# A pooling-mixer layer on one core: the output weights of three of seven Strassen products stored as float32r pairs when they are folded

## The chip, the cores and the metric

The kernel runs on one core of a Trainium2 chip. Its metric is the device time of one execution in microseconds. TensorE (PE) multiplies matrices, VectorE (DVE), ScalarE (ACT) and GpSimd (POOL) do the element-wise work, and SyncE (SP), like the others, issues transfers between the memory and the on-chip buffers.

## The reference

One layer is computed, of the pooling kind, on x of 4096 frames by 1024 channels, in float32; the final RMSNorm follows.

```python
def trailing_mean(u, window):
    cs = jnp.cumsum(u.astype(jnp.float32), axis=1)
    lagged = jnp.pad(cs, ((0, 0), (window, 0), (0, 0)))[:, :seq]
    ...
    return ((cs - lagged) / count[None, :, None]).astype(u.dtype)

def pool_mixer(h, in_w, group_w, group_b, scale, out_w):
    u, gate = jnp.split(h @ in_w, 2, axis=-1)
    ug = u.reshape(b, s, POOL_GROUPS, POOL_GROUP_DIM)
    pooled = jnp.stack([trailing_mean(ug[:, :, g], w) for g, w in enumerate(POOL_WINDOWS)],
                       axis=2) - ug
    mixed = jnp.einsum('bsgc,gcd->bsgd', pooled, group_w) + group_b
    y = mixed.reshape(b, s, POOL_WIDTH) * scale * jax.nn.silu(gate)
    return y @ out_w

# one layer: h = x + pool_mixer(rms_norm(x)); the result is rms_norm(h)
```

The windows are 2, 4, 8 and 16 frames, one for each group of 256 channels. `in_w` is 1024 x 2048, `out_w` 1024 x 1024.

## The kernel before, in words

**Pairs.** Every float32 operand of a matmul is held as a pair of float32r tiles, a high part (a rounded copy, made on ScalarE) and a low part (the operand less its high part, made on VectorE). A product is the sum of three passes, high by high, high by low and low by high. Making such a pair is called a split; the tiles with the results are called `w` (weights) and `op` (the operand that changes with the block).

**Seven products.** The three big products (values, gate, output) are cut into 2 x 2 quarters and done with seven products instead of eight, P1 to P7 (the scheme of Strassen and Winograd). Each needs a sum or difference of quarters of the weights and of the operand; P1 and P2 take quarters as they are. The weights' sums are made once by `combine` (P5, P4 and P3 among them), stored in memory and loaded where they are used.

**Blocks.** The group maps are multiplied into the value weights at the start, so that what is left of the mixing is the trailing mean. Then come four input blocks of 1024 frames for the first half of the channels ("a", a0 to a3), four for the second half ("b", b0 to b3), each with the values and gates of its channels and with seven products in the order P1, P2, P7, P6, P5, P4, P3; and eight output blocks ("o") of 512 frames, in the order P1, P7, P6, P2, P5, P4, P3. One product of an input block is 48 matmuls of 512 columns and takes 10.4 us; a few products are cut once more into seven smaller ones. The operand sums of later blocks are formed ahead, kept in memory as `sd` (`sd2_1_0` is block 2, P1, first half), loaded into a slot and split into an `op` tile. Beside the products of a block VectorE also adds the banks' results into the quarters, makes the trailing means (a prefix scan, a difference and a scaled subtraction, on `vt` slots with a `window` tile) and gates.

**The output weights.** `load_wo` (L376) loads four raw quarters of one half of `out_w` in b1 and b2. `make_wo` (L381) scales their rows, in step P6 of the same block, and `store_weights` (L303) stores P1 and P2, forms the other five by `combine` and stores those in `wod`, one 512 KB tile for each product and half. This is a fold: the first (half 0) falls into b1, the second (half 1) into b2. In the last input block b3, `load_w` (L387) loads a product's two halves into slots, splits them into its `w` tiles (by then free of the gate's weights) and gives the slots back.

```python
                for p in {P1: (), P2: (), P7: (P1,), P6: (P2, P7), P5: (P6, P5)}.get(i, (i,)):
                    load_w(wod, p)
```

**What sets the order.** There is one instruction queue for each engine, and it runs in order. Which order the instructions stand in is set when the program is built: a scheduler interleaves them by their dependences, `issue_after` ties one behind another, and `InOrder` (L64) keeps the output blocks in the order of the text. Most element-wise work and all DMA issues go through `InOrder.call` and so carry its line, L79, in the profile; the main matmuls carry L799, those of `product_seven` L745, the small leaf products of the mixing L941. Slots are shared: eleven `st`, eight `vt`, four `op`. `take` hands out the one that has been free the longest, and `give` returns it; a tile that is taken again waits for the last reader of the one before.

Of the kernel before, what the change touches and what calls it, by code (L numbers as in the profile page):

```python
# [10 lines left out]
F32 = mybir.dt.float32  # L11
F32R = mybir.dt.float32r
# [3 lines left out]
P = 128  # L16
D = 1024
S = 4096
H = 512
# [12 lines left out]
P1, P2, P3, P4, P5, P6, P7 = range(1, 8)  # L32
# [54 lines left out]
def kernel(  # L87
# [37 lines left out]
    vector, scalar, gpsimd, sync = (  # L125
        InOrder(tc, e) for e in (nc.vector, nc.scalar, nc.gpsimd, nc.sync)
    )
# [5 lines left out]
    dram = ctx.enter_context(tc.tile_pool(name="dram", bufs=1, space=bass.MemoryType.DRAM))  # L133
# [3 lines left out]
    def new_w(i):  # L137
        return [
            mem.tile([P, 2, 2, H], F32R, tag=f"w{i}_{h}", name=f"w{i}_{h}") for h in range(2)
        ]  # L140

    w = {i: new_w(i) for i in (P1, P2, P6, P7)}
# [35 lines left out]
    def take(pattern="p (a b) -> p a b", pool=None, **sizes):  # L178
        sizes = sizes or {"a": 2}
        if pool is None:  # L180
            spare = len(vt.free) > keep[0] or not st.free
            pool = vt if spare and vt.age() < st.age() else st
        return pool.take(lambda t: t[:, 0:D].rearrange(pattern, **sizes))
# [4 lines left out]
    def give(ap):  # L188
        next(p for p in (st, vt, early, early5) if id(ap) in p.used).give(ap)
# [4 lines left out]
    def sub(dst, a, b):  # L194
        return vector.tensor_tensor(out=dst, in0=a, in1=b, op=ALU.subtract)
# [4 lines left out]
    def copy(dst, src, func=AF.Copy):  # L200
        return scalar.activation(dst, src, func)

    def split(dst, src):

        latest_copy[0] = copy(dst[:, 0], src).ins
        latest_split[0] = sub(dst[:, 1], src, dst[:, 0].bitcast(F32)).ins

    latest_split, latest_copy = [None], [None]
# [9 lines left out]
    t3d = [dram.tile([P, 2, H], F32, name=f"t3d{h}") for h in range(2)]  # L218
    wod = {
        i: [dram.tile([P, 2, H], F32, name=f"wod{i}_{h}") for h in range(2)]  # L220
        for i in range(P1, P7 + 1)
    }
    sd = [
        {
# [65 lines left out]
    def combine(b11, b21, b12, b22):  # L290

        sub(b12, b22, b12)
        add(b11, b12, b11)
        sub(b21, b21, b11)
        t1 = take()
        sub(t1, b22, b11)
        return {P6: b11, P7: b12, P5: t1, P4: b21, P3: b22}
# [5 lines left out]
    def store_weights(dst, h, b11, b21, b12, b22):  # L303
        sync.dma_start(out=dst[P1][h], in_=b11)
        sync.dma_start(out=dst[P2][h], in_=b21)
        for i, u in combine(b11, b21, b12, b22).items():
            sync.dma_start(out=dst[i][h], in_=u)
            give(u)


# [65 lines left out]
    def load_wo(h):  # L376
        for n in range(2):
            for kh in range(2):
                raw_wo[kh, n] = load_rows(out_w, 4 * kh + 2 * h, n * H)

    def make_wo(h):  # L381
        us = dict(raw_wo)
        for (kh, n), u in us.items():
            scale_rows(u, pair(scale_c, h, kh))
        store_weights(wod, h, us[0, 0], us[1, 0], us[0, 1], us[1, 1])

    def load_w(src, i):  # L387
        for h in range(2):
            u = take()
            sync.dma_start(out=u, in_=src[i][h])  # L390
            with tc.issue_after(evicted[0]):
                split(w[i][h], u)
            give(u)
# [1274 lines left out]
    def pool_later(n):  # L1668
        kind, b, i = steps[n]
        if i == P4:  # L1670
            args = (b, 0 if kind == "a" else 1, 1, ev.pop("22"), ev.pop("21"))
            wait = int(b == 0) if kind == "a" else 1 if b < NB - 1 else 2
        elif i == P3:
            args = (b, 0 if kind == "a" else 1, 0, ev.pop("12"), ev.pop("11"))
            wait = 1 + int(b == 0) if kind == "a" else 2 if b < NB - 1 else 5
        else:
            return
        pending.append((n + wait, args))

    def pool_due(n):  # L1680
        while pending and pending[0][0] <= n:
            pool(*pending.pop(0)[1])
# [204 lines left out]
    for n in range(2, len(steps)):  # L1887
        kind, b, i = steps[n]
# [78 lines left out]
        if kind in ("a", "b"):  # L1967
            pool_later(n)
            if kind == "a":
                pool_due(n)  # L1970
            if kind == "b" and b == NB - 1:
                for p in {P1: (), P2: (), P7: (P1,), P6: (P2, P7), P5: (P6, P5)}.get(i, (i,)):
                    load_w(wod, p)
            if kind == "b" and b in (1, 2) and i == P7:
                load_wo(b - 1)
            if kind == "b" and b in (1, 2) and i == P6:
                with tc.issue_after(evicted[0]):
                    make_wo(b - 1)
            if kind == "b" and b == NB - 1 and i == P3:
                f = take("p (a b) -> p a b", a=2)  # L1980
                sync.dma_start(
                    out=f.rearrange("p a b -> p (a b)"), in_=final_w.partition_broadcast(P)
                )
                fw.append(f)
# [52 lines left out]
```

## Time and profile before

| what | value |
|---|---|
| median of three runs | 907.41 us (906.5 to 909.38) |
| the profiled execution | 907.14 us |
| its span, first to last instruction | 905.3 us |
| busy TensorE / VectorE / ScalarE / GpSimd | 894.6 / 736.8 / 518.6 / 147.3 us |
| mean granted TensorE clock | 0.998 |
| moved by DMA | 203.30 MB, 225 GB/s on average |

All rows of the profile are from one execution. A row of the table by stretches gives the busy time of each engine in that stretch. A row of the groups gives line, engine, operation, tiles, shape and count, then the sum of busy time and the mean of one, then the idle time of the engine just before them and what ended it. In the rows of a timeline the first number is the start in us from the span's start and the second the time to the end of the row's last instruction; "x3" joins three neighbours. In the rows of DMA issues the last number is the median time from issue to landing.

### The profile page before, as it was taken

What the parts mean: (1) busy time and instruction counts of PE and PEld (TensorE: products, weight loads), DVE (VectorE), ACT (ScalarE), POOL (GpSimd) and SP (SyncE); (2) the same over time, 40 slices, a digit from 0 to 9 for tenths busy, and PEclk for the clock granted to TensorE, in tenths of its full rate; (3) what the DMA queues carried; (4) which work ended last, traced back from release to release, by engine and by line L of the source; (5) the groups of instructions that cost most, each with busy time, mean ns of one, the idle gap of its engine ahead of it and who ended that gap; (6) DMA issues with size and microseconds to landing.
All of it is one profiled execution on the core that took longest, in us unless ns stands there. A gap on an engine that the chain in (4) does not pass through costs nothing.

```text
span 905.3 us, 12421 instructions
## 1 busy us (share of the span) xinstructions
PE 894.6 (99%) x4554; PEld 791.7 (87%) x4554; DVE 736.8 (81%) x910; ACT 518.6 (57%) x848; POOL 147.3 (16%) x244
## 2 busy tenths in 40 slices
PE   9999999999999999999999999999999999999996
PEld 7888888888888888889889889888889898998996
DVE  3899896984996997694596497699898878888798
ACT  7869547446445465346545644855557466565464
POOL 0031110110111000100010011011132343342430
PEclk9999999999999999999999999999999999999999
DMA  9989779677769565245574574756673855945953
GB/s 339 402 313 320 263 279 314 219 299 286 270 248 363 180 236 183 94 163 190 212 244 175 202 262 142 269 188 204 206 220 81 221 176 142 240 143 138 264 179 116
DMA packets 77756, 203.30 MB, mean 225 GB/s; under 512 B 7296, under 2 KB 25088, under 8 KB 77696
## 3 DMA queue, kind: packets, MB, share of 16 engines
q1 hardware_dynamic: 57872, 143.77, 46.0%
q0 software_dynamic: 19104, 57.69, 20.7%
q10 hardware_dynamic: 720, 1.06, 0.3%
q8 instruction: 35, 0.57, 0.3%
q14 instruction: 25, 0.20, 0.1%
HBM read 130.13 MB, written 72.36 MB: 224 GB/s over the span
## 4 chain that ended last, share of the span: by engine, by line
PE 50%; DVE 21%; DMA 10%; issue 6%; ACT 3%; POOL 1%; SPq 0%; DVEq 0%; POOLq 0%; ACTq 0%
PE bank L799 44%; DVE vt L79 8%; DVE st L79 6%; DVE op L79 5%; PE bank L745 3%; DMA vt<-yd 3%; PE bank L941 3%; DMA st<-wvd 2%; ACT op L79 1%; DMA st<-yd 1%; DVE w L79 1%; DMA out<-vt 1%; ACT vt L79 1%; DMA st<-wod 1%; DMA vt<-rd 1%
## 5 line engine op out<-in xcount | busy, mean ns | idle before, releaser
L799 PE MATMUL bank<-op,w 128*128 128x512 f32 x2544 | 550.6, 379 | 0.2 <-ACT st L79 0.2
L799 PEld LDWEIGHTS bank<-op,w 128*128 128x128 f32 x2544 | 480.4, 189 | 68.9 <-ACT st L79 0.6
L799 PE MATMUL bank<-w,op 128*128 128x512 f32 (+1 forms) x1044 | 230.5, 377 | 0.0
L799 PEld LDWEIGHTS bank<-w,op 128*128 128x128 f32 x1044 | 192.3, 189 | 25.0
L79 DVE TENSOR_TENSOR op<-st,op 128x1024 fp32r<-128x1024 f32 x120 | 145.9, 1220 | 60.1 <-ACT op L79 59.7
L79 ACT ACTIVATE op<-st 128x1024 fp32r<-128x1024 f32 x120 | 125.8, 1052 | 86.4 <-PE bank L799 31.2
L79 ACT ACTIVATE op<-vt 128x1024 fp32r<-128x1024 f32 x65 | 68.3, 1053 | 63.0 <-DVE vt L79 40.6
L79 ACT ACTIVATE vt<-bank 128x512 f32<-128x512 f32 (+1 forms) x122 | 67.4, 577 | 43.9 <-PE bank L799 37.8
L79 DVE TENSOR_TENSOR op<-vt,op 128x1024 fp32r<-128x1024 f32 x65 | 78.4, 1218 | 14.2 <-ACT op L79 14.1
L79 DVE TENSOR_TENSOR st<-st,st 128x1024 f32<-128x1024 f32 (+1 forms) x47 | 51.3, 1104 | 31.6 <-ACT st L79 16.8
L79 ACT ACTIVATE bank<-bank 128x512 f32<-128x512 f32 (+1 forms) x84 | 41.1, 490 | 53.1 <-PE bank L799 39.5
L79 POOL COPY vt<-tails 128x32 f32<-128x32 f32 x14 | 17.0, 1219 | 301.4 <-ACT tails L79 130.3
L79 ACT ACTIVATE st<-bank 128x512 f32<-128x512 f32 (+1 forms) x62 | 35.6, 588 | 37.5 <-PE bank L799 22.7
L79 DVE TENSOR_TENSOR vt<-bank,vt 128x512 f32<-128x512 f32 (+1 forms) x90 | 51.3, 596 | 6.0 <-PE bank L941 4.6
L79 ACT ACTIVATE st<-st 128x1024 f32<-128x1024 f32 x34 | 35.8, 1055 | 28.6 <-DVE st L79 27.1
L79 DVE TENSOR_TENSOR st<-bank,st 128x512 f32<-128x512 f32 (+1 forms) x72 | 43.7, 622 | 6.0 <-PE bank L941 3.1
L79 POOL DMA_DIRECT2D sd<-st x45 | 24.0, 535 | 125.1 <-DVE st L79 77.9
L941 PEld LDWEIGHTS bank<-w,op 128*128 128x128 f32 x312 | 40.4, 191 | 1.7
L79 DVE TENSOR_TENSOR st<-st,vt 128x1024 f32<-128x1024 f32 (+1 forms) x34 | 39.1, 1168 | 2.7 <-DMA vt<-rd 2.4
L941 PE MATMUL bank<-w,op 128*128 128x256 f32 x312 | 41.1, 275 | 0.0
L79 DVE TENSOR_TENSOR vt<-vt 128x1024 f32<-128x1024 f32 (+3 forms) x43 | 38.2, 890 | 0.2
L79 DVE TENSOR_TENSOR_SCAN vt<-vt,window 128x1040 f32<-128x1040 f32 x16 | 37.7, 2374 | 0.6 <-DMA wod<-vt 0.5
(118 smaller groups left out, 768.5 us busy)
## 6 DMA issues: line engine op xcount, KB each, us to landing
sd<-st POOLq DMA_DIRECT2D x45, 512.0 KB, 4.2
st<-sd SPq DMA_DIRECT2D x42, 512.0 KB, 4.0
st<-in_xt SPq DMA_DIRECT2D x28, 512.0 KB, 7.4
st<-in_x SPq DMA_DIRECT2D x21, 512.0 KB, 7.9
yd<-st SPq DMA_DIRECT2D x20, 512.0 KB, 3.3
vt<-yd SPq DMA_DIRECT2D x17, 512.0 KB, 10.5
st<-wod SPq DMA_DIRECT2D x16, 512.0 KB, 5.1
out<-vt POOLq DMA_DIRECT2D x16, 512.0 KB, 3.5
```

Of the source, the lines that this page charges most:

```text
L79: r = f(*args, **kwargs)
L745: latest[0] = nc.tensor.matmul(cell(n, c).rearrange("p (a s) -> p a s", s=2), x1, x2, start=i == P1 and k + m == 0, stop=k == 1 and m == 2 ...
L799: latest[0] = nc.tensor.matmul(ps, a, b, start=start and n == 0, stop=stop and n == 2, skip_group_check=True).ins
L941: latest[0] = nc.tensor.matmul(ps, x1, x2, start=start and k + n == 0, stop=k == 1 and n == 2, skip_group_check=True,).ins
```

## The change

In a fold, P5, P4 and P3 no longer go to `wod`. Each sum u is split at once: a slot `high` is taken, ScalarE copies u into it as float32r, VectorE subtracts it from u in place, and both are stored in a new array `pairs_d` (two stores of 512 KB instead of one). In b3, `load_w` for these three is one transfer of 1 MB a half, issued by GpSimd straight into the `w` tile, with no slot, no copy and no subtraction. The table of steps changes too: P5's load goes from step P5 to step P4, P4's from P4 to P3; P3's stays. The matmuls are the same in number and kind; the instructions that make TensorE's program are L814 instead of L799 in the new text.

```diff
@@ -218,7 +218,11 @@
     t3d = [dram.tile([P, 2, H], F32, name=f"t3d{h}") for h in range(2)]
     wod = {
         i: [dram.tile([P, 2, H], F32, name=f"wod{i}_{h}") for h in range(2)]
-        for i in range(P1, P7 + 1)
+        for i in (P1, P2, P6, P7)
+    }
+    pairs_d = {
+        i: [dram.tile([P, 2, 2, H], F32, name=f"pair{i}_{h}") for h in range(2)]
+        for i in (P5, P4, P3)
     }
     sd = [
         {
@@ -304,7 +308,15 @@
         sync.dma_start(out=dst[P1][h], in_=b11)
         sync.dma_start(out=dst[P2][h], in_=b21)
         for i, u in combine(b11, b21, b12, b22).items():
-            sync.dma_start(out=dst[i][h], in_=u)
+            if i in dst:
+                sync.dma_start(out=dst[i][h], in_=u)
+            else:
+                high = take()
+                latest_copy[0] = copy(high.bitcast(F32R), u).ins
+                latest_split[0] = sub(u.bitcast(F32R), u, high).ins
+                for v, t in enumerate((high, u)):
+                    sync.dma_start(out=pairs_d[i][h][:, v], in_=t)
+                give(high)
             give(u)
 
 
@@ -386,6 +398,9 @@
 
     def load_w(src, i):
         for h in range(2):
+            if i not in src:
+                gpsimd.dma_start(out=w[i][h], in_=pairs_d[i][h].bitcast(F32R))
+                continue
             u = take()
             sync.dma_start(out=u, in_=src[i][h])
             with tc.issue_after(evicted[0]):
@@ -1969,7 +1984,7 @@
             if kind == "a":
                 pool_due(n)
             if kind == "b" and b == NB - 1:
-                for p in {P1: (), P2: (), P7: (P1,), P6: (P2, P7), P5: (P6, P5)}.get(i, (i,)):
+                for p in {P1: (), P2: (), P7: (P1,), P6: (P2, P7), P5: (P6,), P4: (P5,), P3: (P4, P3)}[i]:
                     load_w(wod, p)
             if kind == "b" and b in (1, 2) and i == P7:
                 load_wo(b - 1)
```

The order of instructions moves at three places. The first is VectorE behind the first fold, where the end of b1 runs into P1 of b2. In these rows `op3` and `op0` are the two halves of that P1's operand; `st9` and `st1`, `vt3` hold the folded sums. Before:

```order
L79 TENSOR_TENSOR vt6_106<-bank7_76,vt6_106 128x512
L79 TENSOR_TENSOR op2_87<-st5_94,op2_87 128x1024
L79 TENSOR_TENSOR op1_86<-vt4_104,op1_86 128x1024
L79 SCALAR_TENSOR_TENSOR vt3_103<-vt0_100,window_3423 128x1040
L79 SCALAR_TENSOR_TENSOR vt7_107<-vt6_106,window_3432 128x1040
L79 TENSOR_TENSOR st6_95<-bank0_69,st6_95 128x512
L79 TENSOR_TENSOR st6_95<-bank1_70,st6_95 128x512
L79 TENSOR_TENSOR op3_88<-st8_97,op3_88 128x1024
L79 TENSOR_TENSOR st2_91<-bank2_71,st2_91 128x512
L79 SCALAR_TENSOR_TENSOR vt3_103<-vt3_103,vt0_100 128x2x512
L79 TENSOR_TENSOR st2_91<-bank3_72,st2_91 128x512
L79 TENSOR_TENSOR op0_85<-st1_90,op0_85 128x1024
```

After, VectorE in the same stretch:

```order
L79 TENSOR_TENSOR vt3_103<-vt3_103,st8_97 128x1024
L79 TENSOR_TENSOR vt6_106<-bank7_76,vt6_106 128x512
L79 TENSOR_TENSOR op2_87<-st5_94,op2_87 128x1024
L79 TENSOR_TENSOR op1_86<-vt4_104,op1_86 128x1024
L79 SCALAR_TENSOR_TENSOR vt7_107<-vt6_106,window_3441 128x1040
L79 TENSOR_TENSOR st1_90<-st1_90,st8_97 128x1024
L79 TENSOR_TENSOR st6_95<-bank0_69,st6_95 128x512
L79 TENSOR_TENSOR st6_95<-bank1_70,st6_95 128x512
L79 TENSOR_TENSOR st2_91<-bank2_71,st2_91 128x512
L79 SCALAR_TENSOR_TENSOR vt3_103<-vt0_100,window_3432 128x1040
L79 TENSOR_TENSOR st2_91<-bank3_72,st2_91 128x512
L79 TENSOR_TENSOR st9_98<-st9_98,st8_97 128x1024
```

and the ten rows of VectorE that follow these after the change:

```order
L79 SCALAR_TENSOR_TENSOR vt3_103<-vt3_103,vt0_100 128x2x512
L79 SCALAR_TENSOR_TENSOR vt7_107<-vt7_107,vt6_106 128x2x512
L79 SCALAR_TENSOR_TENSOR st6_95<-vt3_103,colt_114,st6_95 128x512 x2
L79 SCALAR_TENSOR_TENSOR st2_91<-vt7_107,colt_114,st2_91 128x512 x2
L79 TENSOR_TENSOR op3_88<-st1_90,op3_88 128x1024
L79 TENSOR_TENSOR op2_87<-vt2_102,op2_87 128x1024
L79 TENSOR_REDUCE window_3570<-vt4_104 128x1
L79 TENSOR_REDUCE window_3579<-vt0_100 128x1
L79 SCALAR_TENSOR_TENSOR vt6_106<-vt4_104,window_3570 128x1040
L79 TENSOR_TENSOR op0_85<-st8_97,op0_85 128x1024
```

The three subtractions with `st8` are new. The halves `op3` and `op0` stood among the evictions of `bank0` to `bank3`, `op0` at the end of the first list. Now both stand in the last list, behind the scaled subtractions of the means (into `st6` and `st2`), and between them are the split of another product's half (`op2`), two reductions and a scan.

The second place is SP's queue in the same stretch, where `sd2_1_0` and `sd2_1_1` are the loads of those two halves and `wod` and `pair` the folded weights. Before:

```order
L79 DMA wod3_0_127<-st9_98 128x1024
L79 DMA wod7_0_135<-st8_97 128x1024
L79 DMA wod6_0_133<-vt1_101 128x1024
L79 DMA st8_97<-sd2_1_0_163 128x1024
L79 DMA wod5_0_131<-vt3_103 128x1024
L79 DMA wod4_0_129<-st1_90 128x1024
L79 DMA st9_98<-sd2_2_1_166 128x1024
L79 DMA vt1_101<-sd2_7_0_175 128x1024
L79 DMA st1_90<-sd2_1_1_164 128x1024
```

After, SP's queue there:

```order
L79 DMA wod7_0_129<-st8_97 128x1024
L79 DMA wod6_0_127<-vt1_101 128x1024
L79 DMA vt1_101<-sd2_7_0_175 128x1024
L79 DMA pair5_0_131<-st8_97 128x1024
L79 DMA pair5_0_131<-vt3_103 128x1024
L79 DMA st5_94<-sd2_6_0_173 128x1024
L79 DMA pair4_0_133<-st8_97 128x1024
L79 DMA pair4_0_133<-st1_90 128x1024
L79 DMA pair3_0_135<-st8_97 128x1024
L79 DMA st1_90<-sd2_1_0_163 128x1024
L79 DMA pair3_0_135<-st9_98 128x1024
L79 DMA st8_97<-sd2_1_1_164 128x1024
```

Both loads now stand behind stores of the pairs. `st8` holds the high parts of all three products in turn, so each copy into it comes after the store before it; it then takes the load of the second half.

The third place is GpSimd's queue at the end of the input blocks, with the six new loads among copies of window tails and ahead of the first additions of x (`in_x`) for the output blocks. After:

```order
L79 COPY vt2_102<-tails_116 128x2x16
L79 DMA w5_0_609<-pair5_0_131 128x2048
L79 COPY vt5_105<-tails_116 128x2x16
L79 DMA w5_1_610<-pair5_1_132 128x2048
L79 COPY vt0_100<-tails_116 128x2x16
L79 DMA w4_0_698<-pair4_0_133 128x2048
L79 DMA w4_1_699<-pair4_1_134 128x2048
L79 DMA w3_0_771<-pair3_0_135 128x2048
L79 DMA w3_1_772<-pair3_1_136 128x2048
L79 DMA st5_94<-in_x 128x512
L79 DMA st9_98<-in_x 128x512
L79 DMA st5_94<-in_x 128x512
```

Before, the copies and additions stood there without the loads between them.

## The prediction

> **What bounds the kernel now.** I read the page's busy times first, then the table by stretches of 25 us, then the list of waits of TensorE.
>
> ```profile
> span 905.3 us, 12421 instructions
> PE 894.6 (99%) x4554; PEld 791.7 (87%) x4554; DVE 736.8 (81%) x910; ACT 518.6 (57%) x848; POOL 147.3 (16%) x244
> ```
>
> TensorE is busy for 894.6 of 905.3 us, and the change touches no matmul. So the time after is 894.6 us plus whatever TensorE then idles, plus 1.8 us outside the span (the profiled execution took 907.14 us, 0.27 below the median 907.41). In the next rows the columns are the length of the stretch, then busy PE, PEld, DVE, ACT, POOL, clock, DMA share and GB/s.
>
> ```profile
> 0.00:25.00 25.00, 23.59 (x126) 18.79 (x127) 10.92 (x18) 17.36 (x30) 0.94 (x5) 1.00 0.94 344
> 450.00:475.00 25.00, 25.00 (x118) 21.89 (x117) 24.86 (x27) 10.27 (x16) 2.33 (x2) 1.00 0.76 257
> 600.00:625.00 25.00, 25.00 (x118) 21.89 (x117) 25.00 (x26) 14.04 (x18) 1.84 (x2) 1.00 0.36 122
> 650.00:675.00 25.00, 23.23 (x125) 20.55 (x124) 23.65 (x34) 16.00 (x29) 8.24 (x18) 1.00 0.67 192
> 875.00:900.00 25.00, 23.01 (x139) 20.89 (x138) 24.26 (x56) 11.91 (x27) 2.87 (x6) 1.00 0.39 140
> ```
>
> ```profile
> PE bank L941 <- DVE vt L79: 1.8, 1, 1.8
> ```
>
> TensorE idles 1.4 us at the start, 1.8 us in 650 to 675 (one wait for VectorE) and 2.0 us in 875 to 900; all after 900 (5.3 us) is the tail. Only the 1.8 us can be won. On the other side VectorE is full in 450 to 475 (24.86 of 25): that is the stretch behind the first fold, into which work is moved. A late VectorE there costs TensorE one for one.
>
> **What is removed.** Six high parts on ScalarE and six low parts on VectorE go from the last input block.
>
> ```profile
> L79 DVE TENSOR_TENSOR w<-st,w 128x1024 fp32r<-128x1024 f32 x25 | 29.6, 1218 | 5.5 <-ACT w L79 5.5
> L79 ACT ACTIVATE w<-st 128x1024 fp32r<-128x1024 f32 x25 | 25.5, 1054 | 6.0 <-DVE st L79 2.4 <-DMA st<-wod 2.1 <-PE bank L799 1.4
> L79 DVE TENSOR_TENSOR st<-st,st 128x1024 f32<-128x1024 f32 x37 | 44.5, 1217 | 30.0 <-ACT st L79 16.8 <-DMA st<-wvd 13.1
> L79 ACT ACTIVATE st<-st 128x1024 f32<-128x1024 f32 x34 | 35.8, 1055 | 28.6 <-DVE st L79 27.1 <-DMA st<-in_x 1.4
> ```
>
> That is 6 x 1.218 = 7.3 us of VectorE and 6 x 1.054 = 6.3 us of ScalarE. Both lie beside matmuls, so they are worth nothing by themselves; they count only as far as they pull the 1.8 us wait at 670 forward. The rows before it:
>
> ```profile
> 612.01 51.96 PE L799 MATMUL bank<-w,op 128*128 128x512 f32 x240
> 644.62 0.69 DVE L79 TENSOR_TENSOR st<-st,st 128x512 f32<-128x512 f32 x1 [1.49 <-DMA st<-wod]
> 645.23 0.68 DVE L79 TENSOR_TENSOR st<-bank,st 128x512 f32<-128x512 f32 x1
> 651.27 2.48 DVE L79 SCALAR_TENSOR_TENSOR st<-st,ors,st 128x1024 f32<-128x1024 f32 x2 [0.63 <-POOL ors L79]
> ```
>
> VectorE waits 1.49 us at 644.62 for an inner weight, and that load's tile came free only after a late split. With VectorE some 7 us ahead this wait goes. But the eviction at 645.23 reads the sixth output product (24 matmuls each), which ends at 612.01 + 144 x 51.96/240 = 643.2, and the row scaling at 651.27 hangs on its sums through GpSimd. So what follows moves forward by at most 1.5 us, not 7: the gain is between 0 and 1.5 us, and I take 1.2.
>
> **What is added at the folds.** Each of the two folds gets three copies (3 x 1.055 = 3.2 us of ScalarE), three subtractions (3 x 1.217 = 3.7 us of VectorE) and three more 512 KB stores. Behind each fold comes P1 of the next input block, whose operand halves are split on VectorE out of slots that the fold held. The trace before, first fold:
>
> ```profile
> 427.04 62.33 PE L799 MATMUL bank<-op,w 128*128 128x512 f32 x288
> ```
>
> ```profile
> 448.27 1.22 DVE L79 TENSOR_TENSOR vt<-st,vt 128x1024 f32<-128x1024 f32 x1
> 449.41 1.88 DVE L79 TENSOR_TENSOR vt<-bank,vt 128x512 f32<-128x512 f32 x3
> 451.21 1.21 DVE L79 TENSOR_TENSOR op<-st,op 128x1024 fp32r<-128x1024 f32 x1
> 453.66 4.68 DVE L79 TENSOR_TENSOR_SCAN vt<-vt,window 128x1040 f32<-128x1040 f32 x2
> 458.26 1.26 DVE L79 TENSOR_TENSOR st<-bank,st 128x512 f32<-128x512 f32 x2
> 459.44 1.21 DVE L79 TENSOR_TENSOR op<-st,op 128x1024 fp32r<-128x1024 f32 x1
> 462.90 1.21 DVE L79 TENSOR_TENSOR op<-st,op 128x1024 fp32r<-128x1024 f32 x1
> 464.04 1.40 DVE L79 SCALAR_TENSOR_TENSOR st<-vt,colt,st 128x512 f32<-128x512 f32 x2
> 465.36 1.22 DVE L79 SCALAR_TENSOR_TENSOR vt<-vt,vt 128x1024 f32<-128x1024 f32 x1
> ```
>
> P6, P5, P4 and P3 are 192 matmuls from 427.04 at 62.33/288 = 0.216 us: P1 starts at 468.5. The rows at 459.44 and 462.90 are its two halves; the second is done at 464.1, 4.4 us ahead. These rows also give VectorE's pace from start to start: 1.14 us for a 1024 operation (448.27 to 449.41), 0.60 for an eviction (three from 449.41 to 451.21), 2.30 for a scan (two from 453.66 to 458.26), 0.66 for a 512 one (two from 464.04 to 465.36).
>
> Now the changed order. From the last sum of the fold (vt3, at 448.27 as before, since nothing ahead of it moves) to the second half of P1's operand, VectorE's queue holds ten 1024 operations (the sum, three new subtractions, the two splits for P3, two subtractions of the window means, the first half of P1, the first half of P2), seven evictions, three scans, four 512 operations and two tiny reductions (0.2 us). That is 11.4 + 4.2 + 6.9 + 2.6 + 0.2 = 25.3 us: the second half starts at 473.5 and is done at 474.8. The first half stands 4.7 us ahead of it (itself, P2's half, the reductions, a scan) and is done at 470.0.
>
> TensorE then goes so. At 468.5 it can do one matmul, on the high part; the next reads the low part of half one, at 470.0: **1.4 us** idle. Eight more matmuls (1.7 us) stand before the first that reads the low part of half two, so it is there at 471.8 and waits until 474.8: **3.0 us** idle. The sum is **4.4 us**, in a queue that cannot be reordered when it runs. So the 4.4 us of slack are used up and as much again is lost, from 3.4 us of subtractions and from a pooling scan and mean that the new order puts ahead of P1's halves.
>
> The loads could add to it. One slot takes the high part of all three products, so each copy waits until the store before it has landed, and the loads of P1's halves stand behind these stores in SP's queue.
>
> ```profile
> 447.53 0.90 SPq L79 DMA_DIRECT2D st<-sd  x1
> 455.61 8.85 SPq L79 DMA_DIRECT2D st<-sd  x4
> ```
>
> ```profile
> wod<-st SPq DMA_DIRECT2D x10, 512.0 KB, 2.8
> st<-sd SPq DMA_DIRECT2D x42, 512.0 KB, 4.0
> sd<-st POOLq DMA_DIRECT2D x45, 512.0 KB, 4.2
> st<-in_x POOLq DMA_DIRECT2D x18, 256.0 KB, 7.5
> ```
>
> Before, the halves were issued at 447.5 and 455.6. Now the first needs the store of P4's low part, issued at 458.2 when the second subtraction ends, and so goes out near 462 and lands near 466; the second needs P3's high part stored, and goes out near 465 and lands near 469. Their copies take 1.05 us each and VectorE reaches the halves at 468.8 and 473.5, so both are just in time. A landing 2 us later than the median would lose up to 1 us at the first half; none can come earlier than VectorE does. I put 4.4 to 6.5 us, and take 4.5.
>
> The second fold has another order: no scan stands between P1's halves there.
>
> ```profile
> 520.03 1.22 DVE L79 TENSOR_TENSOR vt<-st,st 128x1024 f32<-128x1024 f32 x1
> 498.80 62.33 PE L799 MATMUL bank<-op,w 128*128 128x512 f32 x288
> ```
>
> From 520.03 there are six 1024 operations, seven evictions and one scan (6.8 + 4.2 + 2.3 = 13.3 us) to the first half, done at 534.5, and 4.6 us more to the second, done at 539.1. P1 starts at 498.80 + 192 x 0.216 = 540.3 and reads the second half 1.3 us later: 2.5 us to spare, cost 0, or up to 2 us if a store there is slow.
>
> **What is moved to GpSimd's queue.** The six loads are now 1 MB each and wait for TensorE to leave the weight tile. Queued behind them are two copies of window tails and then the residual additions.
>
> ```profile
> 595.07 3.81 POOL L79 COPY vt<-tails 128x32 f32<-128x32 f32 x1 [2.10 <-ACT tails L79]
> 621.02 0.94 POOL L79 DMA_DIRECT2D st<-in_x  x1 [22.13 <-DVE st L79]
> ```
>
> P5's tile is free at 591.3 (612.0 less two products of 10.4), before the copy at 595.07 is due; the last, P3's, is free at 612.0, 9 us ahead of the addition at 621.02. No such transfer of 1 MB is in the trace: twice the 512 KB row of this queue is 8.4 us, and four times the accumulating 256 KB row is 30 us. So P3's lands between 621 and 642 and is read at 643.2; I take the first, since it is a plain copy too. Cost 0. The doubled bytes (3.1 MB more) fall where the DMA share is 0.36.
>
> **The sum**: 907.14 + 4.5 - 1.2 = 910.4, 3.3 us above the profiled execution and 3.0 above the median.
>
> **The rivals.**
> (a) Not slower: P1's halves come in time and the wait at 670 goes. The point is the second half's end: by 469.8 TensorE never waits. For it: before, the same place had 4.4 us to spare, against 3.4 us of added subtractions. Against it: the printed order puts a scan and two means ahead, and VectorE was full there already. Time 907.1 - 1.2 = 905.9.
> (b) Slower by more: the 3.0 us gap grows to over 3.4 us by a late load, or the second fold stalls too, and TensorE's clock drops. The trace shows a slow clock at the very start:
>
> ```profile
> L1687 PE MATMUL bank<-const-bfloat16-1.0 128*128 128x512 bf16 x8 | 3.5, 623 | 0.8 <-PEq L2022 0.8
> ```
>
> Eight matmuls in 3.5 us are 0.44 us each against 0.216: a stretch as long costs 1.8 us. The granted clock was 1.00 in 650 to 675 in spite of the 1.8 us wait. With 2 us of late loads and such a stretch, 910.4 + 2 + 1.8 = 914.2. The Trainium skill, "TensorE: Matmul & The Clock Gate", section "HAM oscillation — how this bites in real kernels", says that idle gaps over about 3.4 us throttle the array again; by that rule the gap forecast here stays just under it, and no run here shows one so long.
> (c) The change doesn't hide its loads: P5's or P3's pair comes late in output block 0. It decides only if a landing takes over 30 us; each us beyond is lost, so 911 to 916.
>
> **How the numbers follow.** The forecast (stall of 4.4 to 6.5 us, gain 0 to 1.5) has 0.63, and its own range is 910 to 913.5. Rival (a) has 0.21, (b) 0.12, (c) 0.04. About 0.3% (2.7 us, so 904.7 to 910.1) is what a measurement can tell from no change. The forecast lies just above its edge: a seventh of it (0.09) falls inside, which with 0.17 of (a) makes 0.26 within, and 0.04 of (a) is left for faster. Slower is 0.54 + 0.12 + 0.04 = 0.70. The range 906 to 914 takes in (a) near its middle and most of (b).
>
> **What would show it.** Right: TensorE waits of about 1.4 and 3.0 us for VectorE's op near 469 and 472, none near 540, and the wait at 670 shorter by 1 us or so; VectorE full from 448 to 477; the loads of the pairs landed before 630. Wrong: no wait of TensorE near 470, or one that a DMA ends; the wait at 670 unchanged; a granted clock below 1.00 behind the gap; TensorE waiting for w in output block 0.

## The result, and the profile after

| | median | range | executions |
|---|---|---|---|
| before | 907.79 us | 906.09 to 910.33 | 10 |
| after | 912.11 us | 910.04 to 912.97 | 10 |

The ratio is 1.0043, 95% interval 1.0029 to 1.0056: 3.9 us slower (2.6 to 5.1); the two medians are 4.3 apart. The profiled execution took 911.34 us, 4.2 more than that of before. Its page begins so:

```profile
span 909.3 us, 12433 instructions
PE 895.9 (99%) x4554; PEld 791.8 (87%) x4554; DVE 736.6 (81%) x910; ACT 519.0 (57%) x848; POOL 150.7 (17%) x250
```

VectorE and ScalarE did as much as before (736.6 us for 736.8, 519.0 for 518.6): the six splits were moved, not saved. The list of TensorE's waits after gives whom it waited for, the us in total, how often, and the longest:

```profile
PE bank L814 <- DVE op L79: 4.0, 2, 2.8
...
PE bank L956 <- DVE vt L79: 0.3, 1, 0.3
```

The wait of 1.8 us at 670 is down to 0.3 (now on L956, the same instruction in the longer text), and two waits for `op` are new. The timeline of TensorE after shows where (in square brackets the idle time ahead of the row and what ended it):

```profile
463.83 4.48 PE L814 MATMUL bank<-op,w 128*128 128x512 f32 x20
469.53 1.99 PE L814 MATMUL bank<-op,w 128*128 128x512 f32 x8 [1.22 <-DVE op L79]
474.35 7.82 PE L814 MATMUL bank<-op,w 128*128 128x512 f32 x35 [2.82 <-DVE op L79]
```

Beside the waits the stall costs a little more: the eight matmuls at 469.53 take 1.99 us where eight at 0.216 take 1.73, and the row at 474.35 begins with such a longer matmul too. Set against the trace of before matmul by matmul, TensorE loses 4.6 us at this place: 4.04 of idle time and 0.27 in the first matmul behind each wait.

The timeline of VectorE after gives the two releasers, the first and the last of these rows, and what stood between the halves:

```profile
468.26 1.22 DVE L79 TENSOR_TENSOR op<-st,op 128x1024 fp32r<-128x1024 f32 x1
469.40 1.22 DVE L79 TENSOR_TENSOR op<-vt,op 128x1024 fp32r<-128x1024 f32 x1
470.53 0.23 DVE L79 TENSOR_REDUCE window<-vt 128x1 f32<-128x8 f32 x2
470.79 2.38 DVE L79 TENSOR_TENSOR_SCAN vt<-vt,window 128x1040 f32<-128x1040 f32 x1
473.09 1.20 DVE L79 TENSOR_TENSOR op<-st,op 128x1024 fp32r<-128x1024 f32 x1
```

The halves that ended at 460.7 and 464.1 before end at 469.5 and 474.3, and none of these rows has idle time ahead of it: VectorE was at work all the while, as the table by stretches has it too.

```profile
448.00:477.00 29.00, 24.96 (x115) 21.23 (x114) 28.97 (x30) 13.11 (x19) 2.39 (x2) 1.00 0.78 271
```

The loads of the pairs, on GpSimd's timeline and among the DMA issues (1 MB, median 7.2 us to landing):

```profile
617.08 0.54 POOL L79 DMA_DIRECT2D w<-pair  x1 [4.64 <-PE bank L814]
625.51 0.91 POOL L79 DMA_DIRECT2D st<-in_x  x1 [7.89 <-DMA st<-yd]
```

```profile
w<-pair POOLq DMA_DIRECT2D x6, 1024.0 KB, 7.2
```

The last one starts when TensorE leaves the tile and delays nothing: the addition behind it waits for another transfer.

### The profile page after: what moved, and what is told of

Read it like the earlier page. It is cut to its first block, busy times and chain, and to the rows that moved or that the text cites. A ratio compares the mean times of both kernels' runs of the same rounds, so it can differ in the third digit from the quotient of the medians.

```text
span 909.3 us, 12433 instructions
## 1 busy us (share of the span) xinstructions
PE 895.9 (99%) x4554; PEld 791.8 (87%) x4554; DVE 736.6 (81%) x910; ACT 519.0 (57%) x848; POOL 150.7 (17%) x250
## 4 chain that ended last, share of the span: by engine, by line
PE 75%; DVE 10%; DMA 7%; issue 4%; ACT 3%; POOL 1%; DVEq 0%; POOLq 0%; ACTq 0%; SPq 0%
PE bank L814 68%; DVE vt L79 4%; PE bank L760 3%; DVE op L79 3%; PE bank L956 3%; DMA vt<-yd 3%; DVE st L79 2%; ACT st L79 1%; DMA st<-yd 1%; PE bank L466 1%; DMA st<-in_x 1%; DMA out<-vt 1%; ACT op L79 1%; ACT vt L79 1%; POOL otmp L79 1%
## 5 line engine op out<-in xcount | busy, mean ns | idle before, releaser
L814 PE MATMUL bank<-op,w 128*128 128x512 f32 x2544 | 550.9, 379 | 4.0 <-DVE op L79 4.0
L814 PEld LDWEIGHTS bank<-op,w 128*128 128x128 f32 x2544 | 480.2, 189 | 73.1 <-DVE op L79 4.8
L814 PE MATMUL bank<-w,op 128*128 128x512 f32 (+1 forms) x1044 | 230.5, 377 | 0.0
L814 PEld LDWEIGHTS bank<-w,op 128*128 128x128 f32 x1044 | 192.3, 189 | 25.0
L79 DVE TENSOR_TENSOR st<-st,st 128x1024 f32<-128x1024 f32 (+2 forms) x51 | 56.1, 1113 | 29.2 <-ACT st L79 16.8
L79 ACT ACTIVATE st<-st 128x1024 f32<-128x1024 f32 (+1 forms) x38 | 40.0, 1057 | 34.3 <-DVE st L79 29.5
L956 PEld LDWEIGHTS bank<-w,op 128*128 128x128 f32 x312 | 40.2, 191 | 2.4 <-ACT bank L79 0.8
L956 PE MATMUL bank<-w,op 128*128 128x256 f32 x312 | 41.3, 275 | 0.1
```

Source lines behind the costliest of these rows:

```text
L79: r = f(*args, **kwargs)
L814: latest[0] = nc.tensor.matmul(ps, a, b, start=start and n == 0, stop=stop and n == 2, skip_group_check=True).ins
L956: latest[0] = nc.tensor.matmul(ps, x1, x2, start=start and k + n == 0, stop=k == 1 and n == 2, skip_group_check=True,).ins
```

## The experiments

The theory, Q: the time is lost in VectorE's queue behind the first fold, because three subtractions come into a stretch that is full, and the new order puts the halves of P1 behind a scan and the means. The rivals: S, the second fold or the loads on GpSimd's queue; L, the loads of the halves behind the stores, in one slot; W, what is added costs TensorE wherever it stands. Each ratio is to the kernel before, run beside it; it is close to that of the medians, not the same.

**e1, pairs in the first fold only.**

```diff
-            if i in dst:
+            if i not in pairs_d or h != 0:
                 sync.dma_start(out=dst[i][h], in_=u)
...
-            if i not in src:
+            if i in pairs_d and h == 0:
                 gpsimd.dma_start(out=w[i][h], ...)
```

> Pairs are made only in the first fold (half 0); half 1 goes through wod and is split in the last input block as before. Theory Q (VectorE's queue behind the first fold is the loss): the order behind the first fold is that of the changed kernel, so TensorE waits 1.2 and 2.8 us for VectorE's op near 469 and 472, as there; half of the relief in the last block is left, so the wait at 670 is 0.3 to 1.8 us. Time 3 to 4.4 us above the kernel before, ratio 1.0033 to 1.0048. Rival S (the second fold, or the loads of pairs on GpSimd's queue with twice the bytes, carry the loss): about half of the loss or less is left, ratio 1.001 to 1.002.

915.62 us, 1.0097 (1.0082 to 1.0111): 8.8 us, twice the expected loss. TensorE's waits:

```profile
PE bank L814 <- DVE op L79: 4.0, 2, 2.8
PE bank L956 <- DVE vt L79: 2.8, 1, 2.8
```

The two waits for `op` are there as expected, so the first fold alone makes them. Two things were not: the wait at 670 grew to 2.8 us, and the clock fell after both waits of 2.8 us. In the table by stretches, cut at the borders of the clock's record, the columns are length, busy PE, PEld, DVE, ACT, POOL, clock, DMA share and GB/s:

```profile
471.94:475.35 3.41, 0.59 (x4) 0.52 (x4) 3.41 (x3) 1.28 (x2) 0.00 (x0) 1.00 0.89 362
475.35:478.77 3.42, 3.42 (x10) 2.70 (x9) 3.42 (x5) 0.58 (x1) 0.00 (x0) 0.50 0.86 303
478.77:482.18 3.41, 3.41 (x18) 2.98 (x17) 3.41 (x5) 0.58 (x1) 0.00 (x0) 1.00 0.81 302
```

A stretch of 3.41 us with 2.82 idle is followed by one at half clock, ten matmuls in place of some sixteen, which costs 1.7 us; then the clock is back. The longer wait at 670 comes from VectorE's wait for an inner weight, 1.49 us before:

```profile
652.85 0.69 DVE L79 TENSOR_TENSOR st<-st,st 128x512 f32<-128x512 f32 x1 [3.59 <-DMA st<-wod]
```

In this trace 4.6 us are lost at the stall, 2.3 more than before around 670, and 3.1 in two stretches at half clock. The profiled execution, at 917.35 us, is the slowest of four: the other three lie at 915.5 to 915.6 with mean clocks of 0.996 and 0.997 in place of 0.994. One halved stretch fewer in these would fit; none of them was traced.

**e2, pairs in the second fold only** (the same edit with `h != 1` and `h == 1`).

> Pairs are made only in the second fold (half 1); half 0 goes through wod as before. Theory Q: no wait of TensorE near 469 or 472, none near 540; the wait at 670 between 0.3 and 1.8 us. Time 0 to 1.4 us below the kernel before, ratio 0.9985 to 1.0000. Rival S: a loss of 1 to 2 us stays, ratio 1.001 to 1.002.

908.24 us, 1.0021 (1.0010 to 1.0031), slower than the range expected by Q, and near the loss that S expected. TensorE's waits hold no row for `op`, so the second fold makes no wait near 540, as Q has it. But the relief is missing too:

```profile
PE bank L956 <- DVE vt L79: 1.7, 1, 1.7
```

The profiled execution took 907.15 us, as before (907.14). Matmul by matmul it loses 0.45 us in P7's inner products near 564, which the changed kernel loses too and e1 does not: a small cost of the second fold. So S is right as to a small part. The executions spread from 906.5 to 911.4; no row of the profile shows what the longer ones lost, and that stays open.

**e3, the copies and stores without the subtractions.**

```diff
                 latest_copy[0] = copy(high.bitcast(F32R), u).ins
-                latest_split[0] = sub(u.bitcast(F32R), u, high).ins
```

> As the changed kernel, but the six subtractions of the folds are left out: the second part that is stored is the whole sum, so P5, P4 and P3 of the output get wrong low parts. Copies, stores, slots and loads stay, and so does the one slot for the three high parts. Theory Q by the same count of VectorE's queue: three 1024 operations fewer, with the scan and the means still ahead of the second half; the first half is done at 466, before TensorE needs it, the second at 472.5 against 470.4: one wait of 2.1 us in place of 1.2 and 2.8. Relief at 670 as in the changed kernel. Time 0.4 to 1 us above the kernel before, ratio 1.000 to 1.001. Rival L (the halves wait for their loads behind the stores of pairs, and these for the one slot): the chain of copies and stores is the same, so the waits stay at about 4 us, ratio 1.004.

909.09 us, 1.0027 (1.0016 to 1.0038), above the range expected by Q. This kernel leaves out the low parts of P5, P4 and P3, and keeps the work on ScalarE and SP. TensorE's timeline and the stretches:

```profile
469.70 0.70 PE L813 MATMUL bank<-op,w 128*128 128x512 f32 x2 [0.34 <-ACT op L79]
472.06 10.15 PE L813 MATMUL bank<-op,w 128*128 128x512 f32 x38 [1.65 <-DVE op L79]
```

```profile
468.68:472.09 3.41, 1.42 (x7) 0.59 (x5) 3.38 (x4) 3.01 (x5) 0.00 (x0) 1.00 0.94 341
472.09:475.51 3.42, 3.42 (x8) 2.76 (x9) 3.42 (x5) 0.58 (x1) 0.00 (x0) 0.50 0.73 272
```

The waits are 2.0 us where Q said 2.1 and L 4: three subtractions are worth half of the stall. The rest is put down to the scan and the mean that stayed ahead of the second half; that is read from VectorE's order and not tested alone. The clock fell here after 1.99 us idle in one stretch, which was not expected. The six executions lie in two groups: 908.3 to 908.4 us with a mean clock of 0.997, and 909.8 to 910.4 with 0.995. The profiled one, 909.82, is of the second, so a halved stretch (1.7 us) in half of the executions would part them about so; the median 909.09 lies between the groups and belongs to neither.

**e4, the fold called in step P4 in place of P6.**

```diff
-            if kind == "b" and b in (1, 2) and i == P6:
+            if kind == "b" and b in (1, 2) and i == P4:
```

> All arithmetic, stores and loads of the changed kernel, but each fold is called in step P4 in place of P6, so that the halves of the next P1 are loaded into slots before the fold takes them and are split ahead of most of the fold's subtractions (the second half stands behind two evictions after the first, with no other scan). Theory Q: the second half is done by about 466, 4 us ahead; no wait of TensorE near 469 or 472, nor near 540; the wait at 670 at about 0.3 us as in the changed kernel. Time 1.3 us below the kernel before, ratio 0.998 to 0.9995. Rival W (the 3.7 us of extra subtractions and 3.2 us of copies cost TensorE wherever they stand, as VectorE is full there): ratio 1.002 to 1.004, with waits of TensorE for VectorE at another place after 450.

911.19 us, 1.0047 (1.0035 to 1.0059). The waits at 469 and 472 are gone, and W came true in another place:

```profile
PE bank L814 <- ACT bank L79: 3.3, 1, 3.3
```

ScalarE's timeline shows why. A copy for the next P7 stands in its queue ahead of an eviction that TensorE needs, and waits for a sum on VectorE:

```profile
484.69 1.06 ACT L79 ACTIVATE op<-st 128x1024 fp32r<-128x1024 f32 x1 [7.60 <-DVE st L79]
485.65 0.58 ACT L79 ACTIVATE bank<-bank 128x512 f32<-128x512 f32 x1
```

In the kernel before, the copy ran at 477.75 and the eviction at 479.04, both without a wait for VectorE:

```profile
477.75 1.06 ACT L79 ACTIVATE op<-st 128x1024 fp32r<-128x1024 f32 x1 [0.71 <-PE bank L799]
479.04 0.58 ACT L79 ACTIVATE bank<-bank 128x512 f32<-128x512 f32 x1 [0.24 <-PE bank L799]
```

VectorE's full stretch reaches to 485 (it is busy for 4.75 of the 5 us from 480 in before, for 5.00 here); work put later in it only makes another product late.

**e5 and e6, the folds one step earlier, with and without pairs.** e6 makes the same two edits in the kernel before.

```diff
-            if kind == "b" and b in (1, 2) and i == P7:
+            if kind == "b" and b in (1, 2) and i == P2:
                 load_wo(b - 1)
-            if kind == "b" and b in (1, 2) and i == P6:
+            if kind == "b" and b in (1, 2) and i == P7:
```

> All of the changed kernel's arithmetic, stores and loads, with the raw weights loaded in step P2 and folded in step P7, one product earlier than before. There VectorE had 20 us idle from 410 to 440, and the halves of the next P1 stand one behind the other ahead of both means. Theory Q (the loss is VectorE's queue behind the first fold, and it is lost only where that queue is already full): no wait of TensorE near 469, 472 or 486, none near 540; the wait at 670 at 0.3 us; no window of halved clock before the tail. Time 1.0 to 1.5 us below the kernel before, ratio 0.9975 to 0.999. Rival W (the added work costs TensorE wherever it stands): waits of 2 us or more at another place between 440 and 500, ratio 1.002 to 1.005.

> The kernel before with the same move of the folds (raw weights in step P2, fold in P7) and nothing else: no pairs. Theory Q: the wait at 670 stays at 1.8 us and nothing else changes: ratio 0.999 to 1.001. If the move by itself brought what e5 shows, the ratio would be that of e5.

e5: 909.40 us, 1.0026 (1.0017 to 1.0036). e6: 910.13 us, 1.0039 (1.0026 to 1.0053). The long waits are gone in e5, but short ones came:

```profile
PE bank L760 <- ACT st L79: 1.3, 2, 0.6
PE bank L814 <- DVE op L79: 1.0, 2, 0.5
```

The first row is in e6 as well (L745 there, 1.3, 2, 0.6): the move by itself costs. ScalarE's timeline in e5 shows where, and that of before what stood there:

```profile
420.24 0.38 ACT L79 ACTIVATE st<-bank 128x256 f32<-128x256 f32 x1 [1.02 <-DVE op L79]
```

```profile
419.38 0.38 ACT L79 ACTIVATE vt<-bank 128x256 f32<-128x256 f32 x1
```

An inner eviction of P7 now goes into an `st` slot, and waits 1.02 us for a split on VectorE; before, it went into a `vt` slot and waited for nothing. e6 has the same row. The raw weights, loaded earlier, hold other slots; that this is what moves the eviction to `st` was not tested. Both expectations were wrong on that. Against e6 the pairs are 0.7 us cheaper (the intervals overlap), and e5's wait at 670 is 0.3 where e6's is 2.0.

**e7, the subtractions on GpSimd.**

```diff
-                latest_split[0] = sub(u.bitcast(F32R), u, high).ins
+                gpsimd.tensor_tensor(out=u.bitcast(F32R), in0=u, in1=high, op=ALU.subtract)
```

> As the changed kernel, with the six subtractions of the folds on GpSimd, which is idle there. No row of a trace shows what one costs there. Theory Q by the same count, with three subtractions off VectorE's queue but the scan and means still ahead: the first half done at 468, the second at 471.4 against 470.4: one wait of about 1 us, too short for the clock; relief at 670 as in the changed kernel; ratio 0.999 to 1.001. Rival L (loads behind the stores): GpSimd's subtractions are slower, the one slot is held longer, and the waits are 4 us or more, ended by loads: ratio 1.003 to 1.006.

918.23 us, 1.0133 (1.0115 to 1.0151), far above both expected ranges. Here L holds: of the waits the longest, 4.8 us, ends with a copy on ScalarE whose load had landed late. The second row below is mostly a wait of 2.2 us behind the second fold, which the changed kernel does not have.

```profile
PE bank L814 <- ACT op L79: 4.8, 1, 4.8
PE bank L814 <- DVE op L79: 2.9, 3, 2.2
```

```profile
471.91 1.06 ACT L79 ACTIVATE op<-st 128x1024 fp32r<-128x1024 f32 x1 [4.13 <-DMA st<-sd]
```

The groups of GpSimd give the price, and VectorE's timeline what it does beside it:

```profile
L79 POOL TENSOR_TENSOR st<-st,st 128x1024 fp32r<-128x1024 f32 x4 | 9.5, 2375 | 42.4 <-ACT st L79 42.4
```

```profile
450.78 2.97 DVE L79 TENSOR_TENSOR op<-st,op 128x1024 fp32r<-128x1024 f32 x1
457.21 3.37 DVE L79 SCALAR_TENSOR_TENSOR vt<-vt,vt 128x1024 f32<-128x1024 f32 x1
```

VectorE is not relieved: its operations on two on-chip tiles that run beside one of GpSimd's take 2.97 and 3.37 us in place of 1.2.

**e8, each subtraction of the first fold three times.**

```diff
+                if h == 0:
+                    sub(u, u, high)
+                    add(u, u, high)
                 latest_split[0] = sub(u.bitcast(F32R), u, high).ins
```

> As the changed kernel, with each subtraction of the first fold done three times in turn (less the high part, plus it, less it), so that six operations of 1.14 us are added to VectorE's queue there. Theory Q by the same count (fourteen 1024 operations, seven evictions, two scans, two means of halves, four scaled subtractions: 29.7 us from 448.3): the second half is done at 479.2 and the first at 474.5, so TensorE waits 6.0 and 3.0 us, 4.6 us more than in the changed kernel. The clock: a window of 3.4 us with 2.0 us or more of idle was followed by one window at half clock, 1.7 us; here two to three windows qualify, so 1.7 to 3.4 us come on top. Ratio 1.009 to 1.013. Rival (the loss is the stores and loads, not the subtractions): ratio as of the changed kernel, 1.003 to 1.006.

914.01 us, 1.0076 (1.0063 to 1.0089), a little under the expected range. VectorE's queue came out as counted, the halves end at 474.07 and 478.80 (expected 474.5 and 479.2):

```profile
472.87 1.20 DVE L79 TENSOR_TENSOR op<-st,op 128x1024 fp32r<-128x1024 f32 x1
...
477.58 1.22 DVE L79 TENSOR_TENSOR op<-st,op 128x1024 fp32r<-128x1024 f32 x1
```

TensorE's waits did not: 0.8 and 3.8 us in place of 6.0 and 3.0.

```profile
469.15 1.13 PE L817 MATMUL bank<-op,w 128*128 128x512 f32 x4 [0.82 <-ACT op L79]
474.12 8.16 PE L817 MATMUL bank<-op,w 128*128 128x512 f32 x23 [3.84 <-DVE op L79]
```

The new order lets it do four matmuls on the high part first, and at half clock, which held for two stretches, the next ones lasted until the second half was there:

```profile
469.85:473.26 3.41, 0.43 (x3) 0.03 (x1) 3.41 (x4) 0.06 (x1) 0.00 (x0) 1.00 0.65 184
473.26:476.67 3.41, 2.55 (x6) 2.09 (x7) 3.41 (x4) 1.06 (x1) 0.00 (x0) 0.50 0.98 322
476.67:480.09 3.42, 3.42 (x9) 2.69 (x9) 3.42 (x6) 1.06 (x1) 0.00 (x0) 0.50 1.03 414
480.09:483.50 3.41, 3.41 (x17) 2.98 (x17) 3.41 (x3) 0.53 (x1) 0.00 (x0) 1.00 0.86 297
```

**e9 and e11, the fold tied behind P7's evictions, with and without pairs.** e11 makes the same edit in the kernel before.

```diff
+        behind_fold = evicted[0]
         run(n)
...
-                with tc.issue_after(evicted[0]):
+                with tc.issue_after(behind_fold):
                     make_wo(b - 1)
```

> All of the changed kernel, with the fold still called in step P6 but tied behind the last eviction of the product before (P7) in place of the last one of P6, so that it starts some 10 us earlier, in VectorE's idle time from 428 to 445, and behind P7's inner evictions on ScalarE, which e5 and e6 had disturbed. By the count of VectorE's queue the second half of P1 is done by 464, 6 us ahead. Theory Q: no wait of TensorE near 418, 438, 469, 472, 486 or 540; the wait at 670 at 0.3 us; no window of halved clock before the tail. Time 1.0 to 1.5 us below the kernel before, ratio 0.998 to 0.999. Rival W (what is added behind a product of the input blocks costs TensorE wherever it stands): waits of 1 us or more at other places from 428 to 500, ratio 1.001 to 1.004.

> The kernel before with the tie of e9 and nothing else (no pairs): the control for e9. If e9's gain is the pairs' (the load of the inner weight in output block 0 comes earlier), the wait at 670 is here 1.8 us as before and the ratio 0.9995 to 1.0005. If it is the tie's, the ratio is that of e9, 0.9983.

e9: 905.74 us, 0.9983 (0.9975 to 0.9992), faster than both kernels. e11: 906.88 us, 0.9998 (0.9989 to 1.0007). All of e9's waits of TensorE behind the first 25 us are one row, and VectorE splits both halves in a row, done at 465.0, 3.5 us before P1 begins:

```profile
PE bank L956 <- DVE vt L79: 0.4, 1, 0.4
```

```profile
462.70 2.35 DVE L79 TENSOR_TENSOR op<-st,op 128x1024 fp32r<-128x1024 f32 x2
```

In e11 the wait at 670 is 1.0 us, where 1.8 was expected if the gain were the pairs', and its ratio is that of no change:

```profile
PE bank L941 <- DVE vt L79: 1.0, 1, 1.0
```

So the two measures do not agree on whose the gain is. By the medians, 1.4 us below the kernel before in e9 and 0.3 above it in e11, it is the pairs' (the two intervals only just overlap). By the traces, the tie alone brings 0.7 us of the 1.4 at 670, and the pairs the other half. Both measures have the pairs at no cost once the fold is tied earlier.

**e10, pairs for P3 alone**, with before's table of steps.

```diff
-        for i in (P1, P2, P6, P7)
+        for i in (P1, P2, P4, P5, P6, P7)
...
-        for i in (P5, P4, P3)
+        for i in (P3,)
```

> The fold where it was, and pairs for P3 alone; P5 and P4 go through wod and are loaded in the steps of before. One subtraction a fold is added in place of three, and the last split in the last block is P4's, a product earlier. By the count of VectorE's queue the second half of P1 is done at 463.6, 6 us ahead. Theory Q: no wait near 469 or 472. Theory R (the wait at 670 hangs on the load of an inner weight into the slot that the last split of an output weight gives back, not on the number of splits): it goes to about 0.3 us with the two splits of P3 alone; ratio 0.998 to 0.999. Rival V (the wait at 670 shrinks in proportion to the splits taken from VectorE): 1.3 us of it stay; ratio 0.9995 to 1.0005.

906.88 us, 1.0001 (0.9987 to 1.0015). There is no wait near 469, as Q has it: one subtraction a fold costs nothing. But the wait at 670 is 1.9 us, so theory R, that it hangs on the last split, falls, and V's proportion with it. VectorE waits as before:

```profile
PE bank L956 <- DVE vt L79: 1.9, 1, 1.9
```

```profile
644.24 0.69 DVE L79 TENSOR_TENSOR st<-st,st 128x512 f32<-128x512 f32 x1 [1.67 <-DMA st<-wod]
```

and SP's timeline shows that load issued behind another, ahead of which SP stood idle for 6.9 us, until a store out of a `vt` slot had landed:

```profile
639.57 0.32 SPq L79 DMA_DIRECT2D vt<-wod  x1
639.99 0.38 SPq L79 DMA_DIRECT2D st<-wod  x1
```

In e9 the same load goes out at 635.8. Which slots it meets seems to decide, and these shift with all that was taken earlier; by which rule the pairs of all three products free them sooner was not settled.

**e12, the changed kernel again.**

> The changed kernel, run again. The waits near 469 and 472 are 1.2 and 2.8 us again. Whether the clock falls depends on where the 2.8 us lie in the grid of 3.413 us windows: in the first profile they were cut by a border into 1.42 and 1.83 us and the clock stayed; if a border of this run leaves 2.0 us or more in one window, one window at half clock follows and this execution is 1.7 us longer. Times lie in two groups about 1.7 us apart, the lower 3 to 3.5 us above the fast group of before. Ratio 1.003 to 1.0055. If the clock has nothing to do with it, the times lie in one group and no halved window shows behind the wait.

911.91 us, 1.0056 (1.0042 to 1.0071). TensorE's two waits are 1.23 and 2.81 us again. In this profile too the borders of the clock's record cut them, leaving 1.23, 1.61 and 1.20 us idle in three stretches, and the clock stayed. So the halved stretch was seen in e1, which has the same two waits, and in no trace of the changed kernel itself. Its six executions do lie in two groups, as expected: 910.7 to 911.1 and 912.7 to 913.3, with mean granted clocks of 0.997 in the lower one and 0.997, 0.995 and 0.995 in the upper. The ten executions of the result point the same way: the five below 912 us have 0.997 to 0.999, the five above it 0.995 to 0.997. One halved stretch takes 0.002 off the mean (1.7 of 909 us), so it fits most of the slower ones and not all.

## Why the prediction was right

- **The stall behind the first fold**, the term that decides: 1.4 and 3.0 us were forecast, 1.22 and 2.82 measured, at the two matmuls named, with VectorE's end of the second half at 474.3 against 474.8. With the longer first matmul behind each wait it cost 4.6, where the sum took 4.5; that these two lie so close is luck, since the waits were forecast 0.4 too long and no term had the longer matmuls. The count of the queue from start to start held within 0.5 us. e1 and e2 show that the first fold alone makes it; e3, that the subtractions are half of it, which leaves the other half to the order; e8, that the count of VectorE's queue still holds with six operations more, though TensorE's waits then came out otherwise.
- **The second fold at nothing** held as to the wait near 540: there is none, in either profile or in e2. But it is not quite free: P7's inner products near 564 lose 0.4 to 0.5 us in both profiles and in e2, and nothing in e1 and e9, nor in e3, which leaves the subtractions out.
- **The relief at 670** was taken as 1.2 us and came out at 1.5 (1.8 to 0.3). That it comes from the pairs is only half shown: e11, without pairs, has 0.7 us of it by the tie alone, and e2, e10 and e1 have pairs in part and next to none of it (waits of 1.7, 1.9 and 2.8 us). The reason given, a tile that "came free only after a late split", fell with e10, where the load was late with the last split a product earlier. So the size came out near, and the way to it stays open: that is luck in part.
- **The loads on GpSimd** cost nothing, and took 7.2 us to land (8.4 estimated).
- **The clock** is the step that was mis-sized. Rival (b) had it fall only with a gap of over 3.4 us. It falls with 2.0 us of idle in one stretch of 3.41, so the forecast wait of 3.0 us could bring it already, whenever no border cuts the wait too short. Its price, 1.8 us, was right (1.7).
- **The sum**, 910.4, is 0.9 us under the profiled execution. Of its 4.0 us more of span the two terms make 4.6 - 1.5 = 3.1, where 3.3 was forecast. The rest, 0.9, no term had: some 0.5 is the second fold's near 564, and the rest is spread. That the medians lie 4.3 and 5.3 us above before fits a halved stretch in part of the executions; the times and mean clocks of the result's and e12's executions, and e1's trace, speak for that, and no trace of the changed kernel shows it. The kernel before also has slower executions at 908.6 to 909.7 us, in e12's comparison three of 17, with clocks of 0.995 and 0.996; its wait at 670 leaves 1.77 us idle in one window, just under the point. Whether these lose a window there, no trace shows.

Of the rivals, (a) put the point of no wait at 469.8; by the prediction's own count of nine matmuls from 468.5 it is 470.4, which changes nothing here, as the second half was done at 474.3. Of the variants with all pairs only e9's keeps TensorE from every new wait, and it gives 905.7, near the 905.9 that (a) was priced at.

## What to carry to other kernels

When work is moved off a stretch into another, read from the trace how full the engine's queue is at the new place, and count the new order from start to start up to the operand that the bounding engine reads next: this gave the stall within half a microsecond. A fold that is tied to the end of a step can be tied to an earlier one when the idle time lies there, and the same change then costs nothing or gains. Price a wait together with the clock: here some 2 us of idle time within one window of 3.41 us cost 1.7 more.

## What the runs showed of the hardware

**The clock's window.** In every trace the granted clock changes only at borders a whole number of 3.413 us apart (from the first full clock to the first drop 138.0 of them in e1, 137.0 in e3, 141.0 in e4), and the first border lies at another place of the program in each run. Stretches with 1.99 (e3), 2.79 (e4), 2.82 (e1), 2.98 (e8) and 3.41 us (e7) idle were followed by half clock; those with 1.77 (before), 1.83 (the changed kernel) and 1.86 (e7) were not. So the point lies between 1.86 and 1.99 us, 54 to 58% of a window, and a wait of 2.8 us trips it or not by where the border falls. In e7 and e8 the clock stayed at half for two windows, where the first still had 0.7 and 0.9 us idle; in e4, with 0.55, it was back after one. The Trainium skill, "TensorE: Matmul & The Clock Gate", section "What's actually happening", names this window, 3413 ns and free-running, and the traces agree. The rule of the Trainium skill on the same page, in the section "HAM oscillation — how this bites in real kernels", that there be no idle gap over about 3.4 us, is too lenient by these runs: e3 fell after a wait of 1.65 us and one of 0.34 in the same window.

**GpSimd beside VectorE.** Five of e7's six GpSimd subtractions of two on-chip tiles of 128x1024 took 2.36 to 2.39 us, one 3.36, and a VectorE operation of two such inputs beside the first two took 2.97 and 3.37 in place of 1.2. It is longer by nearly the time that it runs beside the subtraction (1.75 us of 1.89, 2.15 of 2.29); two evictions that read a bank, beside the third, took 1.26 together, as elsewhere. The Trainium skill, "SBUF — State Buffer", section "Who interferes with whom", says that a VectorE operation with both inputs in the on-chip buffer contends with a GpSimd operation that reads it, as its second input comes through a read interface that the two share; these rows agree.
